# Twelve units of the modulation moved from the output projection into the gates

## The chip, the cores and the metric

The kernel runs on one core of a Trainium2 chip. Its time is in device microseconds. Before the change three runs took 1723.61, 1727.01 and 1730.42 us, so the median is 1727.01 us.

## The reference, cut to what matters

One layer of an encoder over 256 tokens of width 2048, in float32. The conditioning vector `c` gives the modulation, six sections of 2048 numbers; the rest of the layer reads them at different times.

```
mod = silu(c) @ ada_w + ada_b             # 2048 x 12288
sh1, sc1, gt1, sh2, sc2, gt2 = split(mod, 6)
h = rms(x, norm1_g) * (1 + sc1) + sh1
u = h @ w_in                               # for the three mixers
ya, yb, yc = neighbourhood attention(u), differential attention(u), gated delta net(u)
gates = sigmoid(h @ gate_w + gate_b)       # three gates of width 2048
merged = gates[0] * (ya @ w_branch_a) + gates[1] * (yb @ w_branch_b) + gates[2] * (yc @ w_branch_c)
x = x + gt1 * (merged @ w_out)
h2 = rms(x, norm2_g) * (1 + sc2) + sh2
x = x + gt2 * ((silu(h2 @ w1) * (h2 @ w3)) @ w2)
```

## The kernel before, in words

**The weight stream.** All weights but those of the modulation come as one list of 128 x 128 tiles, eight to a "half" of 512 KB, 538 halves in all (`stream_plan`). For each half a transfer is issued on SP's queue into one of six `raw` buffers; ScalarE casts it to a rounded copy `wh` (`conv_hi`) and VectorE makes the rest `wl = raw - wh` (`conv_lo`). TensorE multiplies with both. A half is converted two halves ahead of its use (`LA`), and two more are already being loaded. By number of the half the stages are: the combined projection 0 to 113, gate `ga` from 114, branch product `pa` from 146, `gb` with `pb` from 154, gate `gc` from 194, `pc` from 226, the output projection `out` from 242, the first two matrices of the feed-forward `f1` and `f3` from 274 and its last, `f2`, from 450 to the end.

**The units of the modulation.** The modulation doesn't run on TensorE. A unit (`unit`, lines 258 to 272) loads 128 x 1024 weights of `ada` (512 KB, on SP's queue, into the same six `raw` buffers, there named `araw`), and VectorE multiplies them with the broadcast conditioning vector `sb` and sums each row into one column of `part`: one instruction and a short read of its accumulator. A section has 32 units; behind its last unit two short additions make its 16 columns of `mod`. There are 192 units. The first 64 belong to the projection's start. The next 96 make three sections in the order `gt1`, `sh2`, `sc2`, and the last 32 make `gt2` beside the feed-forward. `gt1` is first read where the output projection's sums are taken out of PSUM, `sc2` and `sh2` where `h2` is made at the end of it.

**Where units are issued.** `spread(units, c0, c1)` hangs unit i on half `c0 + i * (c1 - c0) // n`. When the loop comes to a half it first issues the units that hang there and then the conversions. The 96 are cut at `ADA_MID`: the first part lies on halves 132 to 193 (from the tenth column group of `ga` to the end of `gb`), the second on 194 to 225 (`gc`), the rest on 242 to 265 (three quarters of the output projection).

**The side work.** The two attentions and the delta net are generators (`da_side` and `gdn_main` above all). After each product with `wl` the loop may run one step of them (`run_side`); the number a step yields (the table `W`) says how many products lie before the next one. In the first gates this is the end of the differential attention (softmax over maps `s`, their difference `a`, its transposes on TensorE) and then the delta net: `gdn_prep` (`d`, `A`), seven levels of a triangular inverse (`gdn_inverse`: `q`, `of`, `X`, `Y`) and the products that follow (`kk`, `vb`, `uu`, `kq`). Their links alternate between TensorE and VectorE or ScalarE. GpSimd only subtracts in `X`.

**Order.** TensorE's instructions are chained in program order (`chain("pe", ...)`), so a side product whose operand is late holds all that follow. On VectorE and ScalarE the order is pinned only at the very start (`pin`); after that the planner of the framework decides, from its own costs, and what it writes is fixed in the program. Each engine then runs its list in order.

Of the kernel before, what the change touches and what calls it, by code (L numbers as in the profile page):

```python
# [27 lines left out]
ORDERS = [ALT, [(0, 0), (1, 0), (0, 1), (1, 1)] + ALT[4:], [(0, 0), (0, 1), (1, 1), (1, 0)] + ALT[4:]]  # L28

SHORT = 8  # L30
ADA_AT, ADA_MID = 9, (64, 84)

W = dict(col=4, tok=3, kn=6, s=2, sm=12, sm2=22, pt=5, av=3, gs=21, gt=5, dec=3, prep=3, a=8, x0=9,
         l1=8, l2=6, l3=10, kv=18, uu=6, sw=5, so=6, go=2, conv=2, z=9, sqn=8, pgn=1, sqd=8, pgd=2,
# [1284 lines left out]
```

## Time and profile before the change

| | |
|---|---|
| median of three runs | 1727.01 us |
| the profiled execution | 1726.81 us, span 1725.0 us |
| TensorE, products | 1697.1 us busy, 98% |
| VectorE | 1260.1 us busy, 73% |
| ScalarE | 850.6 us busy, 49% |
| transfers | 393.11 MB, mean 228 GB/s |
| granted TensorE clock, mean | 0.997 of full speed |

Busy times are sums over an engine's instructions. Products on TensorE are pipelined, and two of them can overlap in the record, so a busy TensorE isn't TensorE at its peak; its idle time, though, is time without any product. Nearly all instructions are recorded under the lines of two helpers (157 for VectorE and ScalarE, 166 and 169 for TensorE), so they are told apart by the names of tiles: `sd` is a PSUM bank of the side work, `mm` one of the stream. In a row of the timeline the square brackets give the idle time in front of the instruction and what ended it.

### The profile page before, as it was taken

Reading aid. Unit: us, or ns where it says so; the run is one execution under the profiler, and the core shown is the slowest. Engines: PE = TensorE matmul, PEld = TensorE weight load, DVE = VectorE, ACT = ScalarE, POOL = GpSimd, SP = SyncE. Lnnn points to the kernel's source line nnn. Section 1 sums busy time; section 2 is a strip of 40 time slices with the busy share of each in tenths; the row PEclk is TensorE's granted clock in tenths of the full one; section 3 lists DMA queues with packets and bytes.
Section 4 is the critical chain, followed back from the end, with each engine's and each line's share of the span. In section 5 each row is a group of like instructions: output and inputs, shape, how many; then the busy total and the mean of one; then the engine's idle time right before and its main releaser. Section 6 shows DMA issues by size and latency. Waiting matters only on the chain.

```text
span 1725.0 us, 28004 instructions
## 1 busy us (share of the span) xinstructions
PE 1697.1 (98%) x11013; PEld 1534.5 (89%) x11013; DVE 1260.1 (73%) x1894; ACT 850.6 (49%) x1248; POOL 38.3 (2%) x25
## 2 busy tenths in 40 slices
PE   8999999999999999999999999999999999999999
PEld 6999999998889898899898888888888888888887
DVE  6898777986999889876878776666666666545453
ACT  4444445566673444434745554454444444443433
POOL 0000000000003100300000000000000000000000
PEclk9999999999999999999999999999999999999999
DMA  9999964554687775766768566766767666556662
GB/s 331 322 343 328 336 220 150 184 182 136 200 289 244 246 265 188 253 210 208 256 217 269 186 207 222 230 224 228 227 226 228 223 227 225 198 195 202 197 200 95
DMA packets 109431, 393.11 MB, mean 228 GB/s; under 512 B 12146, under 2 KB 14450, under 8 KB 109300
## 3 DMA queue, kind: packets, MB, share of 16 engines
q1 hardware_dynamic: 106852, 389.08, 67.0%
q10 hardware_dynamic: 2448, 2.25, 0.4%
q8 instruction: 86, 1.41, 0.3%
q14 instruction: 45, 0.37, 0.1%
HBM read 389.19 MB, written 2.10 MB: 227 GB/s over the span
## 4 chain that ended last, share of the span: by engine, by line
PE 84%; DVE 9%; DMA 4%; issue 2%; ACT 1%; DVEq 0%; ACTq 0%
PE mm L166 76%; PE sd L166 7%; DMA araw<-ada 3%; DVE wl L157 3%; DVE araw L157 3%; PE sd L169 1%; DVE d L157 1%; DVE ga L157 0%; DMA raw<-wst 0%; DVE Y L157 0%; DVE gb L157 0%; DVE s L157 0%; ACT wh L157 0%; DVE q L157 0%; ACT bm L157 0%
## 5 line engine op out<-in xcount | busy, mean ns | idle before, releaser
L157 DVE TENSOR_TENSOR wl<-raw,wh 128x1024 fp32r<-128x1024 f32 x538 | 663.7, 1235 | 321.5 <-ACT wh L157 318.4
L157 ACT CAST wh<-raw 128x1024 fp32r<-128x1024 f32 x538 | 565.2, 1052 | 632.5 <-PE mm L166 331.2
L166 PE MATMUL mm<-hp,wh 128*128 128x256 f32 (+1 forms) x2336 | 574.1, 328 | 5.4 <-ACT hp L157 2.9
L166 PE MATMUL mm<-h,wh 128*128 128x512 f32 x1408 | 487.1, 393 | 1.1 <-DVE h L157 1.1
L166 PE MATMUL mm<-hp,wl 128*128 128x256 f32 x1552 | 423.9, 282 | 0.0
L166 PEld LDWEIGHTS mm<-hp,wh 128*128 128x128 f32 x2336 | 385.1, 191 | 34.7 <-issue 6.4
L166 PE MATMUL mm<-h,wl 128*128 128x256 f32 x1408 | 387.7, 279 | 0.0
L166 PEld LDWEIGHTS mm<-h,wh 128*128 128x128 f32 x1408 | 261.8, 187 | 59.2 <-issue 1.4
L166 PEld LDWEIGHTS mm<-hp,wl 128*128 128x128 f32 x1552 | 296.4, 191 | 11.9 <-issue 3.6
L157 DVE SCALAR_TENSOR_TENSOR araw<-araw,sb 128x1024 f32<-128x1024 f32 x192 | 237.2, 1240 | 91.0 <-DMA araw<-ada 90.8
L166 PEld LDWEIGHTS mm<-h,wl 128*128 128x128 f32 x1408 | 265.2, 188 | 2.5
L166 PE MATMUL mm<-hid,wh 128*128 128x512 f32 x704 | 243.2, 392 | 0.0
L166 PE MATMUL mm<-hid,wl 128*128 128x256 f32 x704 | 193.8, 279 | 0.0
L166 PEld LDWEIGHTS mm<-hid,wh 128*128 128x128 f32 x704 | 130.8, 187 | 28.5
L166 PEld LDWEIGHTS mm<-hid,wl 128*128 128x128 f32 x704 | 132.6, 188 | 1.3
L166 PE MATMUL mm<-m,wh 128*128 128x512 f32 (+1 forms) x272 | 89.9, 384 | 0.8 <-DVE po L157 0.8
L166 PE MATMUL mm<-m,wl 128*128 128x256 f32 x256 | 70.9, 280 | 0.0
L166 PEld LDWEIGHTS mm<-m,wh 128*128 128x128 f32 x272 | 49.7, 188 | 11.8 <-DVE po L157 1.1
L762 POOL TENSOR_TENSOR X<-X,of 128x512 f32<-128x512 f32 x20 | 37.5, 1888 | 708.4 <-ACT of L157 604.3
L166 PE MATMUL sd<-hp,wh 128*128 128x256 f32 x256 | 50.9, 289 | 0.0
L166 PEld LDWEIGHTS mm<-m,wl 128*128 128x128 f32 x256 | 48.3, 189 | 0.5
L166 PE MATMUL mm<-yc,wh 128*128 128x256 f32 x256 | 46.2, 283 | 0.0
(252 smaller groups left out, 1519.3 us busy)
## 6 DMA issues: line engine op xcount, KB each, us to landing
raw<-wst SPq DMA_DIRECT2D x538, 512.0 KB, 4.2
araw<-ada SPq DMA_DIRECT2D x192, 512.0 KB, 4.5
x<-xT SPq DMA_DIRECT2D x8, 512.0 KB, 7.3
out<-x ACTq DMA_DIRECT2D x16, 128.0 KB, 3.0
nab<-nab SPq DMA_DIRECT2D x2, 512.0 KB, 6.9
cst<-cst SPq DMA_DIRECT2D x1, 896.0 KB
vec<-vec ACTq DMA_DIRECT2D x1, 152.0 KB, 2.3
lam<-lamv SPq DMA_DIRECT2D x1, 128.0 KB, 3.3
```

Of the source, the lines that this page charges most:

```text
L157: i = f(*a, **k)
L166: return chain("pe", nc.tensor.matmul(*a, **k))
L169: return chain("pe", nc.tensor.transpose(*a))
L762: nc.gpsimd.tensor_tensor(sel(X, b), sel(X, b), nat(of[:], b), op=ALU.subtract)
```

## The change

The two cut points of the 96 units move from 64 and 84 to 72 and 96. Halves 132 to 193 then hold 72 units (64 before), halves 194 to 225 hold 24 (20 before), and the output projection holds none (12 before).

```diff
-ADA_AT, ADA_MID = 9, (64, 84)
+ADA_AT, ADA_MID = 9, (72, 96)
```

The lines that read it stay as they are:

```
    spread(rest[:ADA_MID[0]], first[("ga", ADA_AT)], first[("gc", 0)])
    spread(rest[ADA_MID[0]:ADA_MID[1]], first[("gc", 0)], first[("pc", 0)])
    spread(rest[ADA_MID[1]:], first[("out", 0)], first[("out", 12)])
```

## Rows read from the trace of the kernel before

**Rows 1.** The page's first part: busy us (share of span) xinstructions.
```profile
PE 1697.1 (98%) x11013; PEld 1534.5 (89%) x11013; DVE 1260.1 (73%) x1894; ACT 850.6 (49%) x1248; POOL 38.3 (2%) x25
```

**Rows 2.** Table by stretches: first two gates, third gate, output projection.
```profile
core 0: us, PE busy (x) PEld busy (x) DVE busy (x) ACT busy (x) POOL busy (x), PEclk, DMA share, GB/s
439.00:727.00 288.00, 275.94 (x1902) 251.19 (x1901) 263.44 (x410) 146.64 (x233) 31.10 (x16) 0.99 0.73 244
727.00:842.00 115.00, 115.00 (x741) 102.46 (x740) 84.20 (x116) 54.60 (x75) 6.43 (x4) 1.00 0.65 216
...
893.00:981.00 88.00, 87.23 (x511) 76.44 (x510) 67.20 (x101) 43.41 (x64) 0.00 (x0) 1.00 0.77 253
```

**Rows 3.** Timeline of TensorE: start, length, instruction, idle before and its end.
```profile
481.53 0.63 PE L169 MATMUL sd<-cst,a 128*128 128x128 f32 x4 [2.67 <-DVE a L157]
...
514.75 0.63 PE L169 MATMUL sd<-cst,q 128*128 128x128 f32 x4 [0.25 <-DVE q L157]
...
525.70 1.13 PE L166 MATMUL sd<-X,q 128*128 128x128 f32 x8
...
552.03 1.13 PE L166 MATMUL sd<-X,q 128*128 128x128 f32 x8
...
647.37 0.49 PE L166 MATMUL sd<-kq,uu 128*128 128x128 f32 x2 [1.18 <-DVE uu L157]
...
650.63 0.60 PE L166 MATMUL sd<-kq,uu 128*128 128x128 f32 x4
...
677.61 0.98 PE L169 MATMUL sd<-cst,q 128*128 128x128 f32 x4 [2.92 <-DVE q L157]
...
912.22 0.50 PE L166 MATMUL mm<-m,wh 128*128 128x512 f32 x1 [0.77 <-DVE po L157]
```

**Rows 4.** Timeline of VectorE: units (`araw`) and the links behind them.
```profile
440.34 1.23 DVE L157 SCALAR_TENSOR_TENSOR araw<-araw,sb 128x1024 f32<-128x1024 f32 x1
...
475.27 1.24 DVE L157 SCALAR_TENSOR_TENSOR araw<-araw,sb 128x1024 f32<-128x1024 f32 x1
...
493.91 1.22 DVE L157 SCALAR_TENSOR_TENSOR araw<-araw,sb 128x1024 f32<-128x1024 f32 x1
...
500.87 1.23 DVE L157 SCALAR_TENSOR_TENSOR araw<-araw,sb 128x1024 f32<-128x1024 f32 x1 [0.24 <-DMA araw<-ada]
...
522.23 1.21 DVE L157 SCALAR_TENSOR_TENSOR araw<-araw,sb 128x1024 f32<-128x1024 f32 x1
...
524.82 1.30 DVE L157 TENSOR_TENSOR q<-sd,cst 128x512 f32<-128x512 f32 x2
...
547.11 1.21 DVE L157 SCALAR_TENSOR_TENSOR araw<-araw,sb 128x1024 f32<-128x1024 f32 x1
...
551.20 0.68 DVE L157 TENSOR_TENSOR q<-sd,cst 128x512 f32<-128x512 f32 x1
...
599.73 1.23 DVE L157 SCALAR_TENSOR_TENSOR araw<-araw,sb 128x1024 f32<-128x1024 f32 x1 [1.49 <-DMA araw<-ada]
...
648.71 1.22 DVE L157 SCALAR_TENSOR_TENSOR araw<-araw,sb 128x1024 f32<-128x1024 f32 x1
...
649.85 0.69 DVE L157 TENSOR_TENSOR uu<-uu,sd 128x512 f32<-128x512 f32 x1
...
683.31 1.20 DVE L157 SCALAR_TENSOR_TENSOR araw<-araw,sb 128x1024 f32<-128x1024 f32 x1
...
687.44 1.22 DVE L157 SCALAR_TENSOR_TENSOR araw<-araw,sb 128x1024 f32<-128x1024 f32 x1
```

**Rows 5.** Costliest groups, 439 to 727 us: busy us, mean ns | idle before, releaser.
```profile
L157 DVE SCALAR_TENSOR_TENSOR araw<-araw,sb 128x1024 f32<-128x1024 f32 x68 | 86.1, 1266 | 23.7 <-DMA araw<-ada 23.6
```

**Rows 6.** Chain of waits: start us, length us, what was waited for.
```profile
648.82 4.28 DMA araw<-ada
```

**Rows 7.** Table by stretches around the two longest waits; columns as in rows 2.
```profile
480.00:485.00 5.00, 3.47 (x20) 3.12 (x21) 4.45 (x10) 2.81 (x7) 0.00 (x0) 1.00 0.90 327
677.00:679.00 2.00, 1.39 (x6) 1.32 (x7) 2.00 (x3) 0.00 (x0) 0.00 (x0) 0.68 0.18 74
679.00:681.00 2.00, 2.00 (x11) 1.90 (x10) 2.00 (x4) 0.41 (x1) 0.00 (x0) 0.50 0.35 106
```

## The prediction

> **What bounds the kernel now.** I read the page's busy times first: TensorE is busy 98% of the span, VectorE 73% [rows 1]. On that alone work on VectorE is free. The table by stretches says where it is not [rows 2]. The first two gates with their side work (439 to 727 us) have TensorE busy 275.94 of 288 us and VectorE 263.44, so TensorE stands idle for 12.06 us and VectorE for 24.56. The third gate (727 to 842) has no idle TensorE at all and VectorE at 84.20 of 115. The output projection (893 to 981) has TensorE busy 87.23 of 88 and VectorE 67.20 of 88. So VectorE runs at 91% in the stretch that receives eight units, at 73% in the one that receives four, and at 76% in the one that gives twelve.
>
> Next I asked the timeline of TensorE which of its idle times end on whom [rows 3]. In the first stretch the long ones all end on a side result of VectorE: 2.67 us before the transposes of `a`, 2.92 before those of `q`, 1.18 before the products with `uu`; those of over 1 us on `Y` are of the same kind. None ends on the weights' halves `wl`. TensorE therefore isn't slowed by the stream but by links of the attention and delta-net chains that stand in VectorE's queue behind units and conversions. The timeline of VectorE shows those queues [rows 4], and the list of costly groups in the same stretch gives the other half: VectorE's idle time there before units is 23.7 us, 23.6 of it waiting for their own transfers [rows 5]. VectorE is either working or waiting at the head of its queue for a unit's data. The chain of waits goes that way too, through a transfer of `ada` that took 4.28 us at 648.82 [rows 6].
>
> **The change part by part.** Durations are from the profiled execution, 1726.81 us with a span of 1725.0; it is 0.2 us under the median of the three runs, so no correction is made.
>
> Where the units come. The stretch runs from half 132 to 193, 62 halves. With 64 units the formula gives two to halves 132 and 163 and one to every other; with 72 it gives a second unit also to halves 138, 144, 150, 156, 169, 175, 181 and 187, and takes none away anywhere. Counting units in VectorE's order from the first (440.34), those halves hold the 8th, 14th, 20th, 26th, 40th, 46th, 52nd and 58th, which start at 475.27, 493.91, 522.23, 547.11, 599.73, 628.54, 648.71 and 687.44 [rows 4] (of the 64 the first stands there, and seven of these eight). A unit holds VectorE for 1.14 us: the 52nd starts at 648.71 and `uu` behind it at 649.85. Each also issues one 512 KB transfer on SP's queue and takes one of the six `raw` buffers, so the weights' loads queued behind it come one slot later.
>
> What each second unit does, if it falls in beside the one that is there:
> - 475.27: it lies in the softmax chain that leads to `a`, where TensorE already waits 2.67 us [rows 3]. All of it is paid: 1.14.
> - 493.91: VectorE idles 0.24 us at 500.87 and then works through until TensorE waits for `q` at 514.75, which has no slack (0.25 idle already). 1.14 - 0.24 = 0.90.
> - 522.23: two `q` follow at 524.82; the first (half of 1.30 us) is done near 525.5 and TensorE starts on it at 525.70. 1.14 - 0.19 = 0.95.
> - 547.11: `q` at 551.20 ends at 551.88, TensorE starts at 552.03. 1.14 - 0.15 = 0.99.
> - 599.73 and 628.54: behind the first VectorE has just idled 1.49 us for a transfer, and the products that follow are 9 us away; behind the second the next TensorE wait on VectorE is at 647.37, 19 us later. Ends 0 and 1.14 each; I take 0, as no product stands close behind.
> - 648.71: `uu` at 649.85 ends at 650.54, TensorE starts on it at 650.63. 1.14 - 0.09 = 1.05.
> - 687.44: behind the two `q`, and nothing needed soon follows. 0, upper end 1.14.
>
> Sum 5.03 us. A long wait also has a price in clock. After the 2.92 us without a product that end at 677.61 the granted clock was 0.68 and 0.50 in the next two stretches of 2 us, which is 2 x 0.32 + 2 x 0.50 = 1.64 us of lost full-speed work; around the 2.67 us wait it stayed at 1.00 [rows 3, 7]. The first item makes that wait 3.81 us, longer than the one behind which the clock fell to its lower level, so I add 1.64. Ends: 0 (it stays as after 2.67) and 3.28 (one more wait grows as long).
>
> The third gate's four units cost 4 x 1.14 = 4.6 us of VectorE, which has 30.8 idle there, and TensorE waits for nothing [rows 2]. I take 0; with the cover gone it would be 4.6. Their transfers and the eight others are 12 x 0.5 MB. In the first gates the transfers' share goes from 0.73 by the eight's 4.2 MB over 288 us at 244 GB/s to about 0.77, the value that the output projection has now without harm.
>
> The output projection loses twelve units, 12 x 1.14 = 13.7 us of VectorE, but only the wait that is there can be won: 0.77 us before the projection's fifth column group, ending on VectorE [rows 3]. It is the whole idle TensorE of the stretch (88 - 87.23). I take -0.77; the ends are -0.77 and 0, for the four groups finish together and the copies behind them must be made anyhow. The modulation's sums now end in the third gate, before their first reader; nobody waits for them.
>
> Total: 5.03 + 1.64 - 0.77 = +5.9, and 1726.8 + 5.9 = 1732.7 us.
>
> The skill bears on the first gates. There TensorE's busy share (96%) stands above VectorE's (91%), while the weight loads are busy 251.19 of 288 us, 87% [rows 2]. The Trainium skill, "Perfetto Trace Analysis", Identifying the Most-Contended Engine, says that matmul busy time is no good measure for TensorE, that the weight loads' is better, and that occupancy is fair for VectorE. By that rule VectorE is the bound of this stretch and all eight units are paid, the second rival below.
>
> **The rivals.**
> 1. The gates hide the units. For it: VectorE's 23.7 us before units are waits, and a second unit may fill them. Against: they come mostly after 550 us, while four of the five priced places have almost no slack. Then only the projection's gain is left: 1726.8 - 0.77 = 1726.0, with one or two waits grown 1728.
> 2. VectorE with its transfers is the bound of all of the first gates. For it: the long waits all end on it, and the chain goes through its transfers [rows 3, 6]. Against: TensorE is idle only 12 us of 288, so in most places there is some slack. Each of the eight then costs 1.14 plus its share of the waits for transfers, 23.7 / 68 = 0.35: 8 x 1.49 = 11.9, with the clock's 1.64 and -0.77 +12.8: 1739.6. In the worst case a second wait crosses to the low clock as well: 1741.2.
> 3. The other side, faster: the extra units shift their successors out of the chain that ends at 677.61. VectorE's order is the planner's, not the program's, and it already left the units of halves 186 and on behind that chain (none starts in the 15 us before the one at 683.31, in which `q` is made). If the second unit of half 181 pushes one more behind it, that wait shrinks from 2.92 by 1.14 to 1.78 and the clock stays up: -1.14 - 1.64 - 0.77 = -3.6, so 1723.3; with the wait at 481.53 relieved by as much, 1722.1. It decides if more such units leave the chains than enter them. Against: at the five priced places the unit that is there stands ahead of the link.
>
> That the change doesn't do what it says I leave out: the list for the projection is then empty and issues nothing.
>
> **How the numbers follow.** Forecast 0.40 (1729 to 1735.4), hidden 0.22 (1724.5 to 1729), VectorE as the bound 0.27 (above 1735.4), the other side 0.11 (below 1724.5). 0.5% of 1726.8 is 8.6 us, about what a measurement of this kernel can tell from no change: faster is under 1718.2, slower over 1735.4. The second rival lies beyond it: 0.27. Of the third about 0.04 does, as it needs both long waits gone with the lower clock (-2.92 - 2.67 - 1.64 - 0.77 = -8.0, and a little more). 0.69 is left for the same. The range reaches down to 1721, just under the third rival's 1722, and up to 1743, above the second's worst with a unit of the third gate uncovered; some 0.14 is left out.
>
> **What would show it.** Right: between 439 and about 730 us TensorE's idle time grows from 12 to about 17 us, the wait before the transposes of `a` near 481 is over 3.5 us with a granted clock under 1 behind it, and waits of about 1 us on `q` and `uu` appear near 515, 526, 552 and 651. The third gate still has no idle TensorE, and the wait at 912 in the projection is gone. Wrong: idle time that stays at 12 us (the first rival), grows past 22 us with waits for transfers before the added units (the second), or falls while the one before 677.61 shrinks (the third). A third gate with idle TensorE, or a projection that gets shorter by more than 1 us, would refute the terms that I set at 0 and -0.77.

## The result and the profile after

The changed kernel takes 1743.62 us (median of four runs, 1741.06 to 1745.37) against 1725.61 of the kernel before in the same comparison: a ratio of 1.0101, interval 1.0086 to 1.0115. It is slower by about 17 us, close to three times the forecast's 5.9 and 0.6 us beyond the end of the range. The profiled execution took 1743.65 us with a span of 1741.9, and the first part of its page differs little from [rows 1]:

```profile
PE 1701.7 (98%) x11013; PEld 1535.0 (88%) x11013; DVE 1267.4 (73%) x1894; ACT 848.2 (49%) x1248; POOL 37.2 (2%) x25
```

The counts are equal, so nothing was added: the 16.9 us by which the span grew are 4.6 us more of busy time for the same products (1697.1 to 1701.7) and 12.3 us of new idle time on TensorE. Since TensorE's order is the same in both kernels, one instruction can be found in both timelines, and the difference of its two start times is the lag so far. I took five such instructions as borders and asked for the table by stretches between them. First the kernel before (first gates, third gate, branch product `pc`, output projection; columns as in [rows 2]):

```profile
470.67:725.50 254.83, 242.77 (x1702) 223.20 (x1701) 233.06 (x358) 124.55 (x194) 31.10 (x16) 0.99 0.74 248
725.50:841.60 116.10, 116.10 (x749) 103.47 (x747) 84.36 (x117) 55.57 (x76) 6.43 (x4) 1.00 0.65 215
841.60:890.16 48.56, 47.73 (x391) 47.05 (x390) 39.30 (x67) 28.68 (x39) 0.00 (x0) 1.00 0.67 229
890.16:987.21 97.05, 95.23 (x549) 82.89 (x548) 73.93 (x114) 47.59 (x70) 0.00 (x0) 1.00 0.74 244
```

and the same work in the kernel after:

```profile
470.08:733.40 263.32, 246.12 (x1702) 224.25 (x1700) 246.16 (x374) 124.45 (x195) 30.21 (x16) 0.99 0.77 255
733.40:857.08 123.68, 118.01 (x747) 103.40 (x747) 87.65 (x125) 52.28 (x72) 6.28 (x4) 1.00 0.67 218
857.08:908.35 51.27, 48.28 (x390) 47.29 (x391) 41.87 (x70) 31.63 (x44) 0.00 (x0) 1.00 0.64 220
908.35:1004.07 95.72, 94.67 (x550) 82.75 (x548) 61.58 (x88) 46.57 (x70) 0.00 (x0) 1.00 0.56 186
```

Length minus the first busy time is TensorE's idle time:

| stretch | length | of it idle TensorE |
|---|---|---|
| first gates | +8.49 | 12.06 to 17.20 |
| third gate | +7.58 | 0 to 5.67 |
| `pc` | +2.71 | 0.83 to 2.99 |
| output projection | -1.33 | 1.82 to 1.05 |

What of a length isn't idle time is busy time of the same products; the third gate's part of it (116.10 to 118.01) comes at a granted clock of 1.00 in both kernels. Up to the first border the new kernel is 0.59 us ahead; behind the last one nothing more is gained or lost (the lag there is 1004.07 - 987.21 = 16.86). The surprise is the second line. The stretch that had no idle TensorE at all lost nearly as much as the first gates, and it isn't VectorE's occupancy that explains it: VectorE is busy 87.65 of 123.68 us there, 71%.

The waits in the timeline of TensorE of the kernel after that answer to [rows 3], and the new ones (start, length, instruction, idle before and its end):

```profile
478.28 0.51 PE L166 MATMUL mm<-hp,wl 128*128 128x256 f32 x2 [0.57 <-DVE wl L157]
480.90 0.63 PE L169 MATMUL sd<-cst,a 128*128 128x128 f32 x4 [1.76 <-DVE a L157]
...
518.60 0.63 PE L169 MATMUL sd<-cst,q 128*128 128x128 f32 x4 [3.18 <-DVE q L157]
...
530.63 1.23 PE L166 MATMUL sd<-X,q 128*128 128x128 f32 x8 [0.87 <-DVE q L157]
...
567.05 1.16 PE L166 MATMUL sd<-Y,d 128*128 128x128 f32 x8 [1.46 <-DVE Y L157]
...
655.53 0.60 PE L166 MATMUL sd<-kq,uu 128*128 128x128 f32 x4
...
674.09 1.16 PE L166 MATMUL sd<-uc 128*128 128x128 f32 x8 [1.42 <-ACT qg L157]
...
684.41 0.63 PE L169 MATMUL sd<-cst,q 128*128 128x128 f32 x4 [3.01 <-DVE q L157]
...
739.95 1.13 PE L166 MATMUL sd<-X,q 128*128 128x128 f32 x8 [1.70 <-DVE q L157]
...
816.79 0.49 PE L166 MATMUL sd<-kq,uu 128*128 128x128 f32 x2 [1.14 <-DVE uu L157]
...
843.79 0.50 PE L166 MATMUL mm<-hp,wl 128*128 128x256 f32 x2 [1.50 <-DVE wl L157]
```

In the first gates the long waits moved rather than grew everywhere. In the third gate all of them are new and all end on VectorE; the last is even a conversion of the weight stream, `wl`, which never held TensorE there before.

What VectorE did instead is shown by its own waits. First the kernel before, its third gate (what was waited for: us in total, times, longest us):

```profile
DVE araw L157 <- DMA araw<-ada: 19.9, 13, 4.8
```

then the kernel after, first the third gate (735 to 862 us), then the first gates (439 to 735), where [rows 5] had 23.6:

```profile
DVE araw L157 <- DMA araw<-ada: 35.8, 18, 4.2
...
DVE araw L157 <- DMA araw<-ada: 17.3, 14, 2.4
```

The units' waits for their own transfers nearly doubled in the third gate, and fell in the first gates. The end of the third gate shows what one costs (timelines of VectorE and, in the one row `wh`, of ScalarE, of the kernel after):

```profile
826.18 1.23 DVE L157 SCALAR_TENSOR_TENSOR araw<-araw,sb 128x1024 f32<-128x1024 f32 x1 [4.18 <-DMA araw<-ada]
...
827.67 2.35 DVE L157 TENSOR_TENSOR wl<-raw,wh 128x1024 fp32r<-128x1024 f32 x2
...
833.63 1.23 DVE L157 SCALAR_TENSOR_TENSOR araw<-araw,sb 128x1024 f32<-128x1024 f32 x1 [3.60 <-DMA araw<-ada]
...
836.04 1.05 ACT L157 CAST wh<-raw 128x1024 fp32r<-128x1024 f32 x1 [0.27 <-PE mm L166]
...
840.70 1.23 DVE L157 SCALAR_TENSOR_TENSOR araw<-araw,sb 128x1024 f32<-128x1024 f32 x1 [1.85 <-DMA araw<-ada]
...
842.52 1.22 DVE L157 TENSOR_TENSOR wl<-raw,wh 128x1024 fp32r<-128x1024 f32 x1
```

These units stand at the head of VectorE's queue for up to 4.18 us without working, and what is behind them in the list stands too, ready or not. Behind the third, TensorE waits 1.50 us at 843.79 for the `wl` that VectorE could only begin at 842.52. Counting conversions in order, the `wh` that this one subtracts is the one at 836.04: it was done 5.4 us earlier. The unit at 833.63 was asked for at 828.91 (its issue on SP's queue), 4.7 us earlier; the page's last part gives 4.5 us from issue to landing for `araw<-ada`, in both kernels.

Why was it asked for so late? The issue came when the first of the two `wl` at 827.67 was done. SP's own waits, of its unit issues (line 260), tell the same; first the third gate before, then after:

```profile
SPq L260 <- DVE wl L157: 9.4, 8, 2.3
SPq L260 <- DVE araw L157: 7.9, 5, 3.6
SPq L260 <- DVE gc L157: 7.5, 3, 4.2
...
SPq L260 <- DVE araw L157: 20.8, 9, 3.9
SPq L260 <- DVE gc L157: 15.3, 4, 5.5
SPq L260 <- DVE wl L157: 9.2, 7, 2.3
```

They went from 24.8 to 45.3 us. So VectorE waits for transfers that had themselves been waiting for VectorE, by the profile's inferred releasers. That this is for a free `raw` buffer fits the program, which has six; no run gives it more of them, so that part is argued.

### The profile page after: what moved, and what is told of

Read it like the earlier page. It is cut to its first block, busy times and chain, and to the rows that moved or that the text cites. A ratio compares the mean times of both kernels' runs of the same rounds, so it can differ in the third digit from the quotient of the medians.

```text
span 1741.9 us, 28007 instructions
## 1 busy us (share of the span) xinstructions
PE 1701.7 (98%) x11013; PEld 1535.0 (88%) x11013; DVE 1267.4 (73%) x1894; ACT 848.2 (49%) x1248; POOL 37.2 (2%) x25
## 4 chain that ended last, share of the span: by engine, by line
PE 78%; DVE 13%; DMA 5%; issue 3%; ACT 1%; DVEq 0%; ACTq 0%; SPq 0%
PE mm L166 72%; PE sd L166 6%; DMA araw<-ada 4%; DVE araw L157 4%; DVE wl L157 4%; DVE d L157 1%; DVE Y L157 1%; DVE ga L157 1%; PE sd L169 0%; DVE gb L157 0%; DVE q L157 0%; DMA raw<-wst 0%; ACT wh L157 0%; DVE s L157 0%; DVE vb L157 0%
## 5 line engine op out<-in xcount | busy, mean ns | idle before, releaser
L157 DVE SCALAR_TENSOR_TENSOR araw<-araw,sb 128x1024 f32<-128x1024 f32 x192 | 241.0, 1260 | 93.1 <-DMA araw<-ada 92.9
L166 PEld LDWEIGHTS mm<-m,wh 128*128 128x128 f32 x272 | 49.6, 188 | 10.3 <-DVE po L157 0.2
```

What stands on the lines that cost most here:

```text
L157: i = f(*a, **k)
L166: return chain("pe", nc.tensor.matmul(*a, **k))
```

## The experiments

**Each cut point by itself.** Is the loss two local ones, or one backlog that the first gates hand on? The first two runs move one cut each.

```diff
-ADA_AT, ADA_MID = 9, (64, 84)
+ADA_AT, ADA_MID = 9, (72, 92)   # e1: eight more in the first gates, third gate as before
+ADA_AT, ADA_MID = 9, (64, 88)   # e2: first gates as before, four more in the third gate
```

> The first gates hold 72 units as after the change, the third gate 20 as before, the output projection 4. Theory 1, the parts add (first gates +8.1 us, third gate and start of pc +11.0, projection -1.6 by the lag of TensorE in the two traces): the first gates' +8 stays and the rest goes, 7 to 8 us over before, and TensorE has under 1 us of idle time in the third gate. Theory 2, one backlog (the late first gates push the third gate's waits): 14 to 17 us over before, with the third gate's waits still there. Theory 3, only a shuffle of the planner's order, no price per unit: anything from -5 to +17, and idle times at places that neither trace shows.

Measured 1732.35 us against 1726.27, ratio 1.0029 (1.0016 to 1.0042). In its trace the lag grows by 5.1 us in the first gates, 1.6 in the third, 0.2 in `pc`, and shrinks by 1.4 in the projection. Its third gate, with 20 units as before (table by stretches, then VectorE's waits for units):

```profile
727.00:843.00 116.00, 115.04 (x743) 102.03 (x742) 83.25 (x115) 51.82 (x71) 8.12 (x5) 1.00 0.65 211
...
DVE araw L157 <- DMA araw<-ada: 30.7, 16, 4.9
```

The waits are nearly as long as after the change, and TensorE idles only 0.96 us: 83.25 of work and 30.7 of waits still fit into 116. The sum of the waits alone is therefore no measure of the loss.

> The first gates hold 64 units as before, the third gate 24 as after, the projection 8. Theory 1 (parts add): 9 to 11 us over before, the waits in the third gate and at the start of pc as after the change. Theory 2 (one backlog, carried from the first gates): 0 to 2 us over before, third gate without idle TensorE. Theory 3 (shuffle): anything from -5 to +17.

Measured 1732.53, ratio 1.004 (1.0026 to 1.0055). Its profiled execution was the longest of its six (1737.41); there the lag grows by 2.6, 7.2, 0.3 and 1.5. The third gate's 7.2 is close to the change's 7.6, with the two longest waits of its second half before the same products (`uu` 1.53 us and `wl` 1.78): its table gives 111.58 busy of 116 us, and VectorE's waits for units rise from 19.9 to 32.5 us.

```profile
727.00:843.00 116.00, 111.58 (x709) 98.52 (x708) 83.33 (x115) 48.85 (x66) 6.27 (x4) 0.99 0.66 215
```

So the third gate's four units cause a loss there without a backlog from in front. How large it is in a usual execution is less sure, as this one is 4.9 us over the median and its 7.2 alone exceeds the median's 6.3 over the kernel before. From 820 to 851 us its granted clock was 0.94, some 1.9 us of full-speed work, where the change kept 1.00; the idle TensorE grew by 4.4. By the medians the two parts sum to 12.3 us, not to 17: they don't add up entirely.

**Units without transfers.** To take the waits away I let the units of this stretch read the broadcast vector alone and issue no transfer.

```diff
+            if 16 <= gi < 19:
+                i = stt(half_sb, half_sb, 0.0, half_sb, op0=ALU.mult, op1=ALU.add,
+                        accum_out=part[:, 96 * u + c:96 * u + c + 1])
...
```

> As before the change, but the 96 units of these stages load nothing: VectorE runs the same instruction over the resident conditioning vector instead, so the modulation for gt1, sh2 and sc2 is wrong. To be read beside e4. If VectorE's working time is what TensorE waits for, 3 us or less are gained over before; if it is the wait for the units' transfers and the buffers they hold, most of the 13.6 us of idle TensorE and 1.6 us of low clock between 470 and 990 us goes: 10 to 15 us under before.

> As after the change, with the same 96 units loading nothing. Theory A, VectorE's working time is the price of the change (12 units, 1.14 us each, in the VectorE-fed stretches): this stays 8 us or more over e3. Theory B, the units' transfers are (a unit at the head of VectorE's queue waits 2 to 4 us for its data, and holds a buffer of the weights): the difference to e3 is 3 us or less.

Measured 1722.38 and 1721.78: ratios 0.9984 (0.9973 to 0.9994) and 0.9977 (0.9968 to 0.9987). This decided nothing. A unit without a transfer has nothing that ties it to its half, and the planner put the 96 units at the same early places in both kernels (from 211 to 638 us), so the cut points no longer changed anything.

**Work without waits, waits without work.** The next four keep the transfers where they are. In one pair a unit multiplies 8 columns instead of 1024, so that its wait is left and its work nearly gone; in the other it works on the broadcast vector at full length, placed behind its transfer in the list but not waiting for it. As nothing reads `raw` there, the buffer doesn't wait for VectorE's multiplication either.

```diff
+            w = 8 if 16 <= gi < 19 else 1024                       # e5, e6: tiny
+            i = stt(raw[:, :w], raw[:, :w], 1.0, sb[:, u * 1024:u * 1024 + w], ...)
...
+            d = nc.sync.dma_start(raw, ada[apos[c], u])            # e7, e8: no wait
+            i = stt(half_sb, half_sb, 0.0, half_sb, op0=ALU.mult, op1=ALU.add, ...)
+            tc.add_manual_dep(i.ins, d.ins.name, nosync, reason="behind its transfer")
```

> As before the change; the 96 units load their 512 KB and wait for them as before, but VectorE works on 8 of the 1024 columns only, so their sums (gt1, sh2, sc2) are wrong. To be read beside e6: VectorE's 1.14 us a unit is gone, its wait for the transfer and the buffer stay. If working time is what TensorE waits for, most of the idle TensorE between 470 and 990 us goes, 10 us under before; if the transfers are, 0 to 5 us under before.

> As after the change, with the same cut to 8 columns. Theory A (VectorE's working time is the price of the change): the difference to e5 falls from 17 us to 4 or less. Theory B (the wait for the units' transfers at the head of VectorE's queue, or the buffers they take from the weights): the difference to e5 stays at 10 us or more.

> As before the change; the 96 units load their 512 KB into the raw buffers, but VectorE's full-length instruction works on the resident vector, placed behind the issue of the transfer without waiting for it (the sums for gt1, sh2 and sc2 are wrong). VectorE's working time, the transfers' traffic and their buffers stay, the wait at the head of VectorE's queue goes. To be read beside e8. If the waits set TensorE's idle time, 8 to 14 us under before; if the working time does, within 3 us of before.

> As after the change, with the same units that don't wait. Theory B1, the wait at the head of VectorE's queue is the price of the change: the difference to e7 falls to 4 us or less. Theory B2, the buffers and the traffic are, or Theory A, VectorE's working time: it stays at 10 us or more (e5 and e6 then tell these two apart).

| | units of before | units of after | difference |
|---|---|---|---|
| work and waits | 1725.61 | 1743.62 | +18.0 |
| work alone (e7, e8) | 1717.31 | 1723.32 | +6.0 |
| waits alone (e5, e6) | 1714.43 | 1711.18 | -3.3 |

The ratios to the kernel before are 0.9921 (0.9903 to 0.9938) for e5, 0.9905 (0.9885 to 0.9925) for e6, 0.9937 (0.9916 to 0.9958) for e7 and 0.9973 (0.9956 to 0.999) for e8. The table by stretches of e7, then of e8, first and third gates:

```profile
439.00:727.00 288.00, 281.73 (x1944) 256.48 (x1943) 272.79 (x417) 148.87 (x236) 33.65 (x18) 0.99 0.71 249
727.00:843.00 116.00, 116.00 (x759) 104.08 (x758) 82.47 (x115) 60.02 (x80) 3.83 (x3) 1.00 0.65 226
```

```profile
439.00:727.00 288.00, 277.47 (x1913) 252.66 (x1912) 282.24 (x432) 146.68 (x233) 30.44 (x16) 0.99 0.74 261
727.00:843.00 116.00, 116.00 (x754) 103.78 (x753) 87.02 (x124) 57.89 (x79) 6.44 (x4) 1.00 0.67 238
```

With the work alone, the first gates' idle TensorE goes from 6.3 to 10.5 us and the third gate has none either way: its 4 x 1.14 us are hidden, as I had said. In e6 VectorE waits 74.3 us for units in the first gates, far more than in any kernel with their work, and TensorE idles only 4.3 (283.73 busy of 288): waits are hidden as well where there is no work. Neither alone costs 17 us. Both stand in one list, and together a unit takes its wait plus its work out of the slack of whatever link is behind it. That reading is argued from the differences: the planner wrote a new list for each of these kernels, so the three differences aren't exact parts of one sum.

**Units held until their data is there.** If the wait at the head of the list is what was missed, the same units without a wait should make the change almost free, with right sums and with buffers that still wait for VectorE. A unit is split: its transfer is issued at its half as before, and the multiplication is hung on the next half and held behind the last `wl` conversion before that, which belongs to the half two further on than the transfer's. The three rest spreads use it.

```diff
+            if early:
+                hooks.setdefault(hx, []).append(u.fetch)       # allocates araw, issues the transfer
+                work.setdefault(hx + 1, []).append(u)          # the multiplication
...
+                tc.add_manual_dep(i.ins, wlast[0].ins.name, nosync, reason="behind its transfer")
```

The first of the four is the other side by itself: fewer units in the first gates (56, 20 and 20), in their old places.

```diff
-ADA_AT, ADA_MID = 9, (64, 84)
+ADA_AT, ADA_MID = 9, (56, 76)
```

> The other way: 56 units in the first gates (64 before), 20 in the third gate as before, 20 in the projection (12 before). If each unit in the first gates has a price that TensorE pays (eight more cost 6 us in e1), eight fewer give back 3 to 6 us, unless the projection, with 20 units of 1.14 us over 67 us of VectorE in 88, begins to wait: then 0 to 3 us. If only the order's accidents count, anything from -5 to +10.

Measured 1732.08, ratio 1.0028 (1.0013 to 1.0042): slower, which only the last of the three expectations (accidents of the order) had allowed. Its profiled execution was the shortest of its ten (1727.61), so its trace doesn't show what the others lose; in it the projection, with 20 units, already loses 2.1 us. This stays open.

> As before the change and with right sums, but each unit's instruction is held behind the conversion of the half two further on (and issued one half after its transfer), so that its data should be there when VectorE comes to it. The wait at the head of VectorE's queue should fall from 52 us between 435 and 1000 us to under 20, and by e7 the time by up to 10 us, to 1717 to 1723. If holding the raw buffers longer starves the weights' transfers it is slower than before, with TensorE waiting for wl.

> As after the change, with the same later units. If the 17 us are the product of waits and working time (e5 to e8: neither alone costs more than 6), the difference to e10 is 3 to 8 us, as between e7 and e8. If the buffers were the cause, it stays at 12 or more.

> Both: 56, 20 and 20 units, each held behind the conversion two halves on. If the two effects add, this is the fastest of all, 1713 to 1720 us; if the waits were the whole price of a unit, it equals e10.

Measured against 1725.84: units of before 1722.24, ratio 0.997 (0.9958 to 0.9982); units of after 1725.04, 0.9996 (0.9984 to 1.0009); 56, 20 and 20 units 1719.68, 0.9958 (0.9943 to 0.9972). The costliest groups of the last, from 439 to 840 us (busy us, mean ns, idle before):

```profile
L157 DVE SCALAR_TENSOR_TENSOR araw<-araw,sb 128x1024 f32<-128x1024 f32 x76 | 99.3, 1307 | 0.0
```

No unit waits there any more, and the price of the change falls from 17 us to 2.8 (1725.04 - 1722.24). The medians stand in the plain order, more units in the first gates being slower: -2.6, 0, +2.8 us for 56, 64 and 72. The other two spreads differ as well, and the step from 64 to 56 isn't clear of the scatter (1718.80 to 1723.13 against 1717.98 to 1722.13), so a price for each unit can't be read from it. The last is the fastest version found that computes all sums, 6.2 us under the kernel before. A multiplication that comes later also holds its `raw` buffer longer; that this would starve the weights is out, since each of the three gained over the same cut in the old places.

**Which stage's waits cause which stage's loss.** Two mixtures with the units of after: only the first gates held late, or only the third gate.

```diff
+    spread(rest[:ADA_MID[0]], first[("ga", ADA_AT)], first[("gc", 0)], True)               # e13
+    spread(rest[ADA_MID[0]:ADA_MID[1]], first[("gc", 0)], first[("pc", 0)], True)          # e14
```

> As after the change, with the later place for the 72 units of the first gates only. If the first gates' waits made their share of the ledger (8 of 17 us, and perhaps by their lag some of the third gate's), this is 8 us or more under after, 1731 to 1736, with the third gate's 5 us of idle TensorE still there. If they also caused the third gate's, 1725 to 1729.

> As after the change, with the later place for the 24 units of the third gate only. If the third gate's waits made their own share (11 us with the start of pc), 1731 to 1735, with the first gates as after the change. If they only pass on what the first gates begin, 1739 or more.

Measured against 1728.17: 1734.93, ratio 1.0035 (1.0021 to 1.005), and 1730.94, ratio 1.0019 (1.0006 to 1.0031). The lag by stretch in e13 is +1.8, +5.5, +2.6 and -1.3, in e14 +6.1, -0.1, +0.6 and -0.8. The third gate of e13, then that of e14, in the table by stretches:

```profile
727.00:843.00 116.00, 112.19 (x720) 98.83 (x719) 83.80 (x116) 50.20 (x69) 7.53 (x4) 1.00 0.69 220
```

```profile
731.00:847.00 116.00, 116.00 (x749) 103.49 (x748) 91.40 (x130) 55.59 (x76) 6.53 (x4) 1.00 0.73 239
```

With the same 24 units, VectorE is even busier in e14 (91.40 against 83.80 us), and TensorE waits for nothing; in e13, where VectorE waits 31.0 us for units there, TensorE loses 3.8. So each stage's loss is caused in it, and in the third gate it is work with waits: without the waits it is gone, by two different edits (e8, e14). Most of the loss in `pc` goes with it (+2.7 to +0.6). The first gates' loss falls from 8.5 to 1.8 when their units are held late, and to 6.1 in e14, where they aren't; the rewritten list alone can thus shift some 2 us. Holding a unit also moves it, and no run moves one without changing its wait.

## Why the prediction was wrong

The direction was right, the size was not, and the range missed by 0.6 us.

The step that failed is "The third gate's four units cost 4 x 1.14 = 4.6 us of VectorE, which has 30.8 idle there, and TensorE waits for nothing [rows 2]. I take 0; with the cover gone it would be 4.6." The idle time that was to be the cover was not free: 19.9 of the 30.8 us were units standing at the head of the list, up to 4.8 us at a time, and I had asked for such waits only in the first gates. The 0 was right for the work (e8, e14) and wrong for work with its waits: +7.6 us in the stretch and most of +2.7 behind it in `pc`, together 10.3, over the upper end of 4.6 that I gave. That end was computed with the work alone; as an estimate afterwards, one more wait of about 4 us (the longest before was 4.8) for each of the four units makes it some 20, and the range would have held the time. A third gate with idle TensorE was the sign that I had set against this term, and it came: 5.67 us.

Work and waits for units, added up, tell the two stages apart better than the busy share did. In the first gates VectorE was full before the change: 263.44 + 23.6 = 287.0 of 288 us [rows 2, 5]. In the third gate it had some 12 us left: 84.36 + 19.9 = 104.3 of 116.1. After the change that gate is full too, at 87.65 + 35.8 = 123.5 of 123.7. The four units brought 3.3 us of work and 15.9 of waits. The sum is no forecast by itself, since added work can also fill waits: in the first gates they fell from 23.6 to 17.3.

The first gates were forecast at 5.03 + 1.64 = 6.7 us and gave 8.5, not far off; but the places did not hold. Of the five priced, one came as worked out: `q` at 525.70, now 530.63, waits 0.87 for 0.95 predicted. `a` waits 1.76, less than the 2.67 before (with 0.57 for a `wl` just ahead of it), and not 3.81; `q` at 514.75, now 518.60, waits 2.93 more for 0.90; `q` at 552.03 and `uu` at 650.63 not at all. The clock's extra loss came out near the 1.64 forecast, but not as forecast. The wait before 684.41 grew to 3.01 and the clock behind it stayed up, where it had fallen in [rows 7]. It fell in two other places instead, around 481, as forecast but not behind a longer wait, and behind the 3.18 us before 518.60. The table of the kernel after around all three, and one row of the kernel before around the second (first):

```profile
520.00:530.00 10.00, 9.47 (x77) 9.27 (x78) 10.00 (x17) 3.18 (x4) 2.47 (x2) 1.00 0.52 179
...
480.00:490.00 10.00, 9.10 (x43) 7.80 (x43) 8.89 (x14) 7.18 (x16) 0.00 (x0) 0.83 0.92 319
510.00:520.00 10.00, 6.82 (x55) 6.65 (x54) 10.00 (x17) 2.10 (x2) 0.00 (x0) 0.96 0.79 254
520.00:530.00 10.00, 9.50 (x68) 9.09 (x66) 10.00 (x16) 2.10 (x2) 0.00 (x0) 0.87 0.47 156
...
684.00:686.00 2.00, 1.59 (x12) 1.53 (x13) 2.00 (x5) 0.00 (x0) 0.00 (x0) 1.00 0.60 236
686.00:688.00 2.00, 2.00 (x17) 1.96 (x16) 2.00 (x4) 1.32 (x2) 0.00 (x0) 1.00 0.44 133
```

Counted as in the prediction, the full-speed work lost there is 10 x (0.17 + 0.04 + 0.13) = 3.4 us, against 1.64 before: 1.8 more. So adding 1.14 us to the wait that stands closest behind a new unit is not a method: a list that is written anew shifts each link by its own amount. The idle total, 12.06 to 17.20, came out as the text said ("from 12 to about 17 us"), and the clock's term too, but with wrong places under both: that is luck.

The output projection's idle time was right: from 1.82 to 1.05 us, -0.77 to the hundredth, with the wait of [rows 3] at 912.22 gone (that product starts at 929.67 with none). The stretch got 1.33 us shorter, though, where more than 1 us was to count against the term; the other 0.56 is busy time (95.23 to 94.67) that the prediction had no term for.

Of the rivals, the first (hidden) and the third (the other side) fall. The second, 1739.6 us, is nearest in time and names the right engine with its transfers, but its 11.9 + 1.64 lay all in the first gates, where 8.5 were measured, and it too set the third gate at nothing. The Trainium skill's rule beside it ("Perfetto Trace Analysis", Identifying the Most-Contended Engine) goes by occupancy. In the first gates the trace agrees that VectorE decides (246.16 of 263.32 us busy, 93%, against 224.25, 85%, for the weight loads); in the third gate it would clear VectorE (71% busy against 103.40 of 123.68 us, 84%, for the weight loads), and there the measurement differs: every new wait of TensorE ends on VectorE.

What stays open: why the two cuts alone sum to 12.3 us and both to 17, why 56 units in the old places are 6 us slower than 64, and whether more `raw` buffers, with transfers issued earlier, would take the waits away as well; that was not run.

## What to carry to other kernels

Here an instruction that was fed by a transfer took, in an engine that runs its list in order, its work plus its wait at that place, and both came out of the slack of the links behind it. So read busy time plus the waits at the head of the queue in the stretch that receives the work, not its busy share alone: 27% idle was little cover when two thirds of it were such waits. If they are there, hold the work behind something that is sure to come after the landing before moving it about; here that was worth some 18 us on the changed kernel, and 3.6 us on the kernel before, 6.2 together with another cut.

## What the runs showed that was not expected

The granted clock didn't follow the length of one wait. It fell to 0.68 and 0.50 behind 2.92 us without a product [rows 7], and to 0.87 over 10 us behind 3.18, but stayed at 1.00 behind 3.01 us in the kernel after. Behind two shorter waits close together, 0.57 and 1.76 us around 480, it was 0.83 over 10 us, where a single one of 2.67 had left it at 1.00. Of the clock's two levels 1.00 is the upper, 2.4 GHz, and 0.50 the lower, 1.2 GHz; a figure between them is a stretch that had both.
